# One dense stop more between the keys' transposes and the state products of the short mLSTM, and two more in its gates' chain

## The chip, the cores and the metric

The kernel runs on one core of a Trainium2 chip. The metric is device time in microseconds (us) of one launch. Engine names are those of the profile: PE is the matrix engine, PEld its weight loads, DVE the vector engine, ACT the scalar engine, POOL the general engine, SP the queue that issues most transfers. Lines (L1578) are lines of the kernel before, unless the text says that a row is from the changed kernel.

## What is computed

One hybrid encoder layer on two inputs: a prompt of 1024 tokens (sequence 0, "short") and a sample of 2048 tokens (sequence 1, "long"), each with 16 learned meta tokens in front. Width 1024, all float32, matrix products split into high and low parts (three products each).

```python
def _encoder_layer(h, ...):
    xn = _rmsnorm(h, g_pre)
    proj = xn @ w_in + b_in                       # 6672 columns
    ya = neighbourhood_attention(na_q, na_k, na_v, rpb);  ya = (ya * silu(na_z)) @ w_a
    yb = (mlstm_branch(ml_qk, ml_v, ml_g, ml_o, conv_w, head_g) * silu(ml_z)) @ w_b
    y = (sigmoid(ga) * ya + sigmoid(gb) * yb) @ w_out
    return h + _rmsnorm(y, g_post)
...
def _mlstm_chunkwise(q, k, v, ig, lf):            # per chunk, 4 heads of 128, two directions
    w = exp(a - max(a));  dC = (w * v)^T k;  dn = w k        # state products
    C, n, m = scan(C * fs + isc * dC, ...)                   # states of all chunks
    S = (q k^T) * exp(logD - m_t)                            # scores
    h = (S v + e * C q) / max(|den|, exp(-m_t))
```

## The kernel before, in words

Two streams of work are interleaved by hand on PE. The **dense** stream (`dense`) holds the big projections (`fm_half`, `tm_unit`, `sgates`) and, at the end, six blocks of merge and output projection (`final`: two for the short, four for the long sequence). It is a generator that yields after each piece of some 12 matmuls with a planned cost (`6 * C512` = 1.41 or `12 * C256` = 1.44 of the planner's microseconds). The **sparse** stream (`sparse`) runs mLSTM of the short sequence, neighbourhood attention of the short, mLSTM of the long, neighbourhood attention of the long. It yields planned costs too (`A_D` = 1.63 in the state part, `A_G` = 1.3 in the gates, times 1.15 for the short sequence), and `run` issues dense pieces until the cost is used up. So a `yield A_D` in `ml_states` is a stop at which dense work is put on PE before the next sparse instructions. Whatever dense work is left when the sparse stream ends is issued after it. PE keeps exactly this order; the other engines' orders, and that of SP, are made by a scheduler from dependencies and its own plan, so they change when PE's order does.

In `ml_states`, for each head of the mLSTM and each block of 256 tokens (four blocks and a rest of 16 tokens in the short sequence, eight and a rest in the long):

1. PE transposes the keys `kf` into PSUM (tile `tr`, L1574); ACT copies the high part `kth` (L1577), DVE subtracts for the low part `ktl` (L1578);
2. a stop; the next block's convolution and values split (`conv_b`, `vsplit`);
3. a stop; PE takes the state products (`mm3`, rows L218 to L220 with `sm<-vwh,kth`, `sm<-vwl,kth`, `sm<-vwh,ktl`), the last of each three reading `ktl`;
4. a stop, and the next block's transposes.

In `ml_gates`, `one(d)` works through a chain of small PE transposes, each of which waits for ACT or DVE work on the one before; both directions step together with a stop of `A_G`.

In `ml_outputs`, PE takes the scores (L1703, L1704) from `kh` and `kl`, which ACT (L1665) and DVE (L1666) make from the reloaded keys.

In the attention, the last products (L1288) of a row of heads are copied (L1295), added (L1302), gated (L1304) and stored by SP to a memory tile `ya` (L1305). `yload` loads it again as `yl` (L1850); ACT makes `yh` of it (L1871), DVE the low part (L1855), and `final` multiplies both (L218 to L220 with `pj<-yh`, `pj<-yl`): for each output tile first the four `yb` tiles, then the four `ya` tiles in order. The last of these four, for the last of the six blocks, comes from the very last attention work.

Other dense rows named later: L697 (DVE scales a projection's result in PSUM), L709 (ACT adds its bias), L318 (DVE makes the low part of a weight tile `whl`), L310 (SP loads a prepared weight tile), L415 and L408 (SP loads input tiles), L365 (ACT squares tokens), L534 and L542 (DVE scales and splits the input).

Of the kernel before, what the change touches and what calls it, by code (L numbers as in the profile page):

```python
# [135 lines left out]
A_N, A_D, A_A, A_G, A_S = (1.08, 0.93), 1.63, 1.79, 1.3, (1.15, 0.91)  # L136


class K:
# [1169 lines left out]
    def ml_gates(self, s, keep, mp, res):  # L1309
        nc = self.nc  # L1310
        T = SEQLEN[s]
        NC_ = 1 + T // P
        NR = 4 * NC_
        t = lambda n, sh, dt=F32, bufs=1: mp.tile(sh, dt, name=n, bufs=bufs)
        kt = lambda n: keep.tile([P, NC_, 4], F32, name=n, bufs=1)
        gt = t("g_t", [P, NC_, 16])
        for d in range(2):
            nc.gpsimd.memset(gt[:, 0, 8 * d:8 * d + 4], -BIG)
            nc.gpsimd.memset(gt[:, 0, 8 * d + 4:8 * d + 8], 1.0e4)
        nc.sync.dma_start(gt[:NM, 0, :], self.GA[s][0:NM, :])  # L1320
        nc.sync.dma_start(gt[:, 1:, :], self.GA[s][NM:, :].rearrange("(c p) g -> p c g", p=P))
        yield 11.0
        gv = gt.rearrange("p c (d k h) -> p d k c h", d=2, k=2)
        lf = t("g_lf", [P, 2, NC_, 4])
        e = t("g_e", [P, 2, NC_, 4])
        u = t("g_u", [P, 2, NC_, 4])
        fl = lambda x: x.rearrange("p d c h -> p (d c h)")
        for d in range(2):
            nc.scalar.activation(e[:, d], gv[:, d, 1], AF.Abs)
            nc.vector.tensor_scalar(lf[:, d], gv[:, d, 1], 0.0, None, op0=ALU.min)  # L1330
        nc.scalar.activation(fl(e), fl(e), AF.Exp, scale=-1.0)
        ln = t("g_ln", [P, 2, NC_, 4])
        yield A_G
        nc.vector.tensor_scalar(fl(u), fl(e), 1.0, None, op0=ALU.add)
        nc.scalar.activation(fl(ln), fl(u), AF.Ln)
        yield A_G
        nc.vector.tensor_tensor(fl(lf), fl(lf), fl(ln), op=ALU.subtract)
        nc.vector.scalar_tensor_tensor(fl(e), fl(u), -1.0, fl(e), op0=ALU.add, op1=ALU.subtract)
        nc.vector.reciprocal(fl(u), fl(u))
        nc.vector.tensor_tensor(fl(e), fl(e), fl(u), op=ALU.mult)  # L1340
        nc.vector.tensor_tensor(fl(lf), fl(lf), fl(e), op=ALU.add)
        yield A_G

        def one(d):
            l2 = lf[:, d].rearrange("p c h -> p (c h)")
            pb = self.psum("sm", [P, 512])
            nc.tensor.matmul(pb[:, :NR], self.tri[:, d, :], l2, start=True, stop=True)
            bT = t(f"g_b{d}", [P, NC_, 4])
            nc.vector.tensor_copy(bT.rearrange("p c h -> p (c h)"), pb[:, :NR])
            aT = kt(f"g_a{d}")  # L1350
            nc.vector.tensor_tensor(aT, gv[:, d, 0], bT, op=ALU.subtract)
            aTf = aT.rearrange("p c h -> p (c h)")
            yield
            pa = self.psum("sm", [P, 512])
            nc.tensor.transpose(pa[:NR, :P], aTf, self.ident)
            aR = t("g_aR", [NR, P], bufs=2)
            nc.scalar.activation(aR, pa[:NR, :P], AF.Copy)
            yield
            cm = t("g_cm", [NR, P], bufs=2)
            rv = (lambda x: x) if d == 0 else (lambda x: x[:, ::-1])  # L1360
            nc.vector.tensor_tensor_scan(out=rv(cm), data0=rv(aR), data1=rv(aR), initial=-3.0e38, op0=ALU.max, op1=ALU.max)
            end = P - 1 if d == 0 else 0
            pg = self.psum("sm", [P, 512])
            nc.tensor.matmul(pg[0:1, :NR], self.ones[:, 0:1], l2, start=True, stop=True)
            rg = t("g_rg", [1, NR], bufs=2)
            nc.scalar.activation(rg, pg[0:1, :NR], AF.Copy)
            yield
            px = self.psum("sm", [P, 512])
            nc.tensor.transpose(px[0:1, :NR], cm[:, end:end + 1], self.ident[:NR, :NR])
            ra = t("g_ra", [1, NR], bufs=2)  # L1370
            nc.vector.tensor_tensor(ra, px[0:1, :NR], rg, op=ALU.add)
            me = t("g_me", [1, NR], bufs=2)
            mpv = t("g_mp", [1, NR], bufs=2)
            nc.gpsimd.memset(mpv, 0.0)
            yield
            for h in range(4):
                w = slice(h, NR, 4)
                nc.vector.tensor_tensor_scan(out=rv(me[:, w]), data0=rv(rg[:, w]), data1=rv(ra[:, w]), initial=0.0,
                                             op0=ALU.add, op1=ALU.max)
            if d == 0:  # L1380
                nc.vector.tensor_copy(mpv[:, 4:], me[:, :NR - 4])
            else:
                nc.vector.tensor_copy(mpv[:, :NR - 4], me[:, 4:])
            yield
            pm = self.psum("sm", [P, 512])
            nc.tensor.transpose(pm[:NR, 0:1], mpv, self.ident[0:1, 0:1])
            mpc = t("g_mpc", [NR, 1], bufs=2)
            nc.vector.tensor_copy(mpc, pm[:NR, 0:1])
            uR = t("g_uR", [NR, P], bufs=2)
            nc.vector.tensor_scalar(uR, cm, mpc, -1.0, op0=ALU.max, op1=ALU.mult)  # L1390
            nc.sync.dma_start(self.UD[s][d][:, :], uR)
            uend = t("g_ue", [NR, 1], bufs=2)
            nc.vector.tensor_copy(uend, uR[:, end:end + 1])
            nc.scalar.activation(cm, uR, AF.Exp, bias=mpc)
            nc.scalar.activation(aR, aR, AF.Exp, bias=uend)
            fs = t("g_fs", [NR, 1], bufs=2)
            nc.scalar.activation(fs, uend, AF.Exp, bias=mpc)
            yield
            pu = self.psum("sm", [P, 512])
            nc.tensor.transpose(pu[:, :NR], uR, self.ident[:NR, :NR])  # L1400
            em = kt(f"g_em{d}")
            nc.vector.tensor_tensor(em.rearrange("p c h -> p (c h)"), pu[:, :NR], bT.rearrange("p c h -> p (c h)"), op=ALU.subtract)
            nc.scalar.activation(em, em, AF.Exp)
            dg = t("g_dg", [NR, NR], bufs=2)
            nc.vector.tensor_scalar(dg, self.ident[:NR, :NR], fs, None, op0=ALU.mult)
            yield
            for name, x in (("e", cm), ("w", aR)):
                pe = self.psum("sm", [P, 512])
                nc.tensor.transpose(pe[:, :NR], x, self.ident[:NR, :NR])
                eT = kt(f"g_{name}T{d}")  # L1410
                nc.vector.tensor_copy(eT.rearrange("p c h -> p (c h)"), pe[:, :NR])
                out[d][name] = eT
                yield
            pf = self.psum("sm", [P, 512])
            nc.tensor.matmul(pf[:, :NR], self.ones[:NR, :], dg, start=True, stop=True)
            fsb = kt(f"g_fb{d}")
            nc.vector.tensor_copy(fsb.rearrange("p c h -> p (c h)"), pf[:, :NR])
            out[d].update(a=aT, em=em, f=fsb)

        out = [{}, {}]  # L1420
        both = [one(d) for d in range(2)]
        while both:
            both = [x for x in both if next(x, "end") != "end"]
            yield A_G
        res += out
# [85 lines left out]
    def ml_states(self, s, h, g, NB, sts):  # L1511
# [55 lines left out]
        for i in range(N):  # L1567
# [13 lines left out]
            conv_b(i + 1)  # L1581
            vsplit(i + 1)
            yield A_D
            vwh, vwl = vws.pop(i)
            if not c0:
                pd = self.psum("sm", [P, 512])
# [10 lines left out]
            for j in range(CB - 1, -1, -1):  # L1597
# [6 lines left out]
                if cc > 0:  # L1604
                    nc.vector.scalar_tensor_tensor(sts[(cc - 1) // CB][:, (cc - 1) % CB, 130:260], sts[b][:, j, 130:260],
                                                   g[1]["f"][:, 1 + cc, h:h + 1], pd[:, 130:260], op0=ALU.mult, op1=ALU.add)
            yield A_D

    def ml_outputs(self, mp, s, h, g, NB, sts, norms):

# [596 lines left out]
```

## Time and profile before

| | us |
|---|---|
| median of 3 runs (lowest, highest) | 2678.69 (2675.17, 2685.75) |
| the profiled execution's own time | 2675.68 |
| its span on the core | 2673.9 |
| PE busy | 2637.4 |
| DVE busy | 1916.3 |
| ACT busy | 1424.9 |
| granted PE clock, mean | 0.996 |

The span runs from the first to the last instruction. PE's busy time is of interest with its idle time beside it: PE is idle for only 36.5 us in all, some 8 of them at the start. PE takes its instructions in the order of the program, so when one of them waits, all dense work behind it waits too. A row of the timeline reads: start, duration, engine, line, operation, output<-inputs, shapes, count, and in brackets the idle time of the engine before it and what ended it.

### The profile page before, as it was taken

To read this page: it belongs to the slowest core of one execution; us is meant where nothing else is said; L and a number is where in the kernel's file an instruction comes from. 1 tells how busy PE (TensorE), PEld (TensorE's weight loads), DVE (VectorE), ACT (ScalarE), POOL (GpSimd) and SP (SyncE) were. 2 spreads that over 40 slices of the span, in tenths; PEclk is the share of its full clock that TensorE was granted. 3 is DMA by queue.
4 is the path that set the end of the run, shared out by engine and by line. 5 is a ranking of instruction groups with operands and counts; after the bars stand their busy time and mean duration, and the time that the engine had idled before them with its cause. 6 is when DMAs were issued, how large, how long until landed. Compare 5 with 4: busy or idle time off the path is not lost.

```text
span 2673.9 us, 46686 instructions
## 1 busy us (share of the span) xinstructions
PE 2637.4 (99%) x15928; PEld 2329.0 (87%) x15928; DVE 1916.3 (72%) x5070; ACT 1424.9 (53%) x3292; POOL 195.7 (7%) x418
## 2 busy tenths in 40 slices
PE   9999999999999999999999999999999999999998
PEld 7998897899978999888888888887889898989888
DVE  5655678788666878546686776867478989897854
ACT  5423555554445655546665665656365655656521
POOL 0111130011301215000000000000000000000000
PEclk9999999999999999999999999999999999999999
DMA  9899988799866999978889988899899898998965
GB/s 371 330 333 337 331 294 311 276 340 312 300 228 233 355 321 306 322 227 274 259 272 344 371 285 267 267 357 337 281 312 308 285 313 276 288 308 265 343 227 207
DMA packets 393517, 800.47 MB, mean 299 GB/s; under 512 B 50528, under 2 KB 173360, under 8 KB 389440
## 3 DMA queue, kind: packets, MB, share of 16 engines
q1 hardware_dynamic: 361728, 697.24, 77.8%
q0 software_dynamic: 31552, 100.25, 10.1%
q8 instruction: 126, 2.06, 0.3%
q14 instruction: 111, 0.91, 0.1%
HBM read 543.72 MB, written 253.60 MB: 298 GB/s over the span
## 4 chain that ended last, share of the span: by engine, by line
PE 87%; DMA 7%; DVE 4%; ACT 2%; issue 1%; SPq 0%; DVEq 0%; ACTq 0%
PE pj L218 9%; PE pj L220 9%; PE pj L219 9%; PE pj L988 8%; PE pj L990 7%; PE pj L989 7%; PE pj L787 5%; PE pj L789 5%; PE pj L788 5%; PE pj L1954 3%; PE pj L1953 3%; PE pj L1955 3%; PE sm L1288 2%; PE tr L1273 2%; DMA wraw<-wu 2%; DMA whl<-w 1%
## 5 line engine op out<-in xcount | busy, mean ns | idle before, releaser
L218 PE MATMUL pj<-xh,whl 128*128 128x512 f32 (+1 forms) x960 | 369.8, 385 | 5.0 <-DMA whl<-w 3.4
L220 PE MATMUL pj<-xh,whl 128*128 128x512 f32 (+1 forms) x960 | 361.2, 376 | 0.0
L219 PE MATMUL pj<-xl,whl 128*128 128x512 f32 (+1 forms) x960 | 360.5, 375 | 0.2 <-DVE xl L446 0.2
L787 PE MATMUL pj<-whl,xh 128*128 128x256 f32 (+1 forms) x1152 | 328.9, 285 | 0.0
L789 PE MATMUL pj<-whl,xl 128*128 128x256 f32 (+1 forms) x1152 | 325.3, 282 | 0.0
L788 PE MATMUL pj<-whl,xh 128*128 128x256 f32 (+1 forms) x1152 | 324.9, 282 | 0.0
L1953 PE MATMUL pj<-whl,mh 128*128 128x256 f32 x768 | 218.1, 284 | 1.1 <-DMA whl<-w 1.1
L787 PEld LDWEIGHTS pj<-whl,xh 128*128 128x128 f32 x1152 | 217.1, 188 | 0.3
L788 PEld LDWEIGHTS pj<-whl,xh 128*128 128x128 f32 x1152 | 217.0, 188 | 0.2
L789 PEld LDWEIGHTS pj<-whl,xl 128*128 128x128 f32 x1152 | 217.0, 188 | 0.0
L1954 PE MATMUL pj<-whl,mh 128*128 128x256 f32 x768 | 216.2, 282 | 0.0
L1955 PE MATMUL pj<-whl,mlo 128*128 128x256 f32 x768 | 215.4, 280 | 0.0
L218 PEld LDWEIGHTS pj<-xh,whl 128*128 128x128 f32 x960 | 181.4, 189 | 37.1 <-issue 4.8
L220 PEld LDWEIGHTS pj<-xh,whl 128*128 128x128 f32 x960 | 181.3, 189 | 35.1
L219 PEld LDWEIGHTS pj<-xl,whl 128*128 128x128 f32 x960 | 181.8, 189 | 30.5 <-issue 1.0
L988 PE MATMUL pj<-xh,whl 128*128 128x512 f32 x512 | 206.7, 404 | 1.5 <-ACT pj L1005 1.1
L990 PE MATMUL pj<-xh,whl 128*128 128x512 f32 x512 | 202.0, 395 | 0.0
L989 PE MATMUL pj<-xl,whl 128*128 128x512 f32 x512 | 201.0, 393 | 0.0
L1280 DVE TENSOR_TENSOR pts<-tr,pts 96x384 fp32r<-96x384 f32 (+2 forms) x192 | 118.7, 618 | 63.4 <-ACT pts L1275 61.9
L1275 ACT ACTIVATE pts<-tr 96x384 fp32r<-96x384 f32 (+2 forms) x192 | 103.5, 539 | 102.6 <-PE tr L1273 101.8
L218 PE MATMUL pj<-yh,whl 128*128 128x512 f32 x384 | 154.1, 401 | 0.0
L219 PE MATMUL pj<-yl,whl 128*128 128x512 f32 x384 | 151.5, 395 | 0.7 <-DVE yl L1855 0.7
(380 smaller groups left out, 6828.8 us busy)
## 6 DMA issues: line engine op xcount, KB each, us to landing
whl<-w SPq DMA_DIRECT2D x131, 1024.0 KB
whl<-q SPq DMA_DIRECT2D x112, 512.0 KB
w<-whl SPq DMA_DIRECT2D x36, 1024.0 KB
wraw<-wu SPq DMA_DIRECT2D x48, 512.0 KB
gt<-st SPq DMA_DIRECT2D x96, 256.0 KB
tg<-gt SPq DMA_DIRECT2D x96, 256.0 KB
q<-po POOLq DMA_DIRECT2D x26, 512.0 KB, 6.8
xt<-xt SPq DMA_DIRECT2D x24, 512.0 KB
```

What stands on the lines that cost most here:

```text
L218: mm(out, ah, bh, start=start, stop=False)
L219: mm(out, ah, bl, start=False, stop=False)
L220: mm(out, al, bh, start=False, stop=stop)
L787: nc.tensor.matmul(o, xh, wh, start=k == 0, stop=False)
L788: nc.tensor.matmul(o, xh, wl, start=False, stop=False)
L789: nc.tensor.matmul(o, xl, wh, start=False, stop=k == KT - 1)
L988: mm(bank, w[:, 0, k], xh[:, k], start=fresh and k == 0, stop=False, skip_group_check=True)
L989: mm(bank, w[:, 0, k], xl[:, k], start=False, stop=False, skip_group_check=True)
L990: mm(bank, w[:, 1, k], xh[:, k], start=False, stop=k == 3, skip_group_check=True)
L1953: nc.tensor.matmul(o, mh[:, k, xs], wh, start=clear > 0 and k == 0, stop=False)
L1954: nc.tensor.matmul(o, mh[:, k, xs], wl, start=False, stop=False)
L1955: nc.tensor.matmul(o, ml[:, k, xs], wh, start=False, stop=clear < 2 and k == KT - 1)
```

## The change

All edits are for the short sequence alone (`s == 0`):

- `one(d)` in `ml_gates` stops once more before the transpose of `uR` (L1400) and once more before the transposes of `cm` and `aR` (L1409);
- `ml_states` stops twice instead of once between the next block's `vsplit` and the state products, and no longer between the state products and the next block's transposes. The last block (the rest of 16 tokens) leaves the loop by its own stop, so it has one stop more than before.

```diff
@@ ml_gates, one(d)
             nc.scalar.activation(fs, uend, AF.Exp, bias=mpc)
             yield
+            if s == 0:
+                yield
             pu = self.psum("sm", [P, 512])
...
             nc.vector.tensor_scalar(dg, self.ident[:NR, :NR], fs, None, op0=ALU.mult)
             yield
+            if s == 0:
+                yield
             for name, x in (("e", cm), ("w", aR)):
@@ ml_states
             conv_b(i + 1)
             vsplit(i + 1)
             yield A_D
+            if s == 0:
+                yield A_D
             vwh, vwl = vws.pop(i)
...
-            yield A_D
+            if s:
+                yield A_D
```

No instruction is added or taken away; instructions move. In the rows of the changed kernel the same code has higher line numbers (by 2 to 7).

**PE, the second block of head 1 in `ml_states`.** `tr<-ident,kf` are the transposes, `sm<-...` the state products, `pj<-xh,whl` and `pj<-xl,whl` dense matmuls. Before:

```order
L1574 MATMUL tr<-ident,kf 128x128 x2
L218 MATMUL pj<-xh,whl 128x512
L219 MATMUL pj<-xl,whl 128x512
L220 MATMUL pj<-xh,whl 128x512
...
L218 MATMUL sm<-vwh,kth 128x260
L219 MATMUL sm<-vwl,kth 128x260
L220 MATMUL sm<-vwh,ktl 128x260
...
L1574 MATMUL tr<-ident,kf 128x128 x2
```

Now:

```order
L1578 MATMUL tr<-ident,kf 128x128 x2
L218 MATMUL pj<-xh,whl 128x512
L219 MATMUL pj<-xl,whl 128x512
L220 MATMUL pj<-xh,whl 128x512
...
L218 MATMUL sm<-vwh,kth 128x260
L219 MATMUL sm<-vwl,kth 128x260
L220 MATMUL sm<-vwh,ktl 128x260
L1578 MATMUL tr<-ident,kf 128x128 x2
```

Between the transposes and the products stood 18 dense matmuls, now 24; between the products and the next transposes 6, now none. In head 3, whose dense matmuls are 256 columns wide, it was 24 and is 48.

**DVE, the first scores of head 0 in `ml_outputs`.** `kl<-kf,kh` makes the low part of the keys for the scores, `s<-sc` reads the scores' result. Before:

```order
L697 TENSOR_TENSOR pj<-pj,rr 128x512
L1691 SCALAR_TENSOR_TENSOR st<-st,g_fb_3124 128x130 x2
L318 TENSOR_TENSOR whl<-wraw,whl 128x1024
L579 TENSOR_TENSOR po<-pr,po 128x2x512
L1666 TENSOR_TENSOR kl<-kf,kh 128x256
L697 TENSOR_TENSOR pj<-pj,rr 128x512
L1666 TENSOR_TENSOR kl<-kf,kh 128x256
L1711 TENSOR_TENSOR s_3839<-sc,s_3839 128x256
```

Now:

```order
L697 TENSOR_TENSOR pj<-pj,rr 128x512
L1698 SCALAR_TENSOR_TENSOR st<-st,g_fb_3150 128x130
L579 TENSOR_TENSOR po<-pr,po 128x2x512
L697 TENSOR_TENSOR pj<-pj,rr 128x512
L318 TENSOR_TENSOR whl<-wraw,whl 128x1024
L1673 TENSOR_TENSOR kl<-kf,kh 128x256 x2
L1718 TENSOR_TENSOR s_3875<-sc,s_3875 128x256
```

The first `kl` stood ahead of the last L697 before the scores; now it stands behind that L697 and an L318. That L697 scales the dense result which PE finishes directly before the scores. ACT's order moves in the same way: `kh` now stands behind the bias of that same result (L709).

**PE, where the attention of the long sequence ends.** `sm<-pts,vt` are the last products of the attention, `pj<-whl,mh` the output projection of the fifth block of `final`, `pj<-yh,whl` the first products of the sixth and last. Before:

```order
L1953 MATMUL pj<-whl,mh 128x256
L1954 MATMUL pj<-whl,mh 128x256
L1955 MATMUL pj<-whl,mlo 128x256
L1288 MATMUL sm<-pts,vt 128x256 x3
L1953 MATMUL pj<-whl,mh 128x256
```

Now:

```order
L1960 MATMUL pj<-whl,mh 128x256
L1961 MATMUL pj<-whl,mh 128x256
L1962 MATMUL pj<-whl,mlo 128x256
L1288 MATMUL sm<-pts,vt 128x256 x3
L218 MATMUL pj<-yh,whl 128x512
L219 MATMUL pj<-yl,whl 128x512
L220 MATMUL pj<-yh,whl 128x512
```

Before, 84 matmuls of the fifth block still stood between the last L1288 and the first product of the sixth block; now there is none.

## Prediction

> **What bounds the kernel now.** I read the page's shares first, then the list of what PE waits for, then the timeline around each of those waits, and the windows with the granted clock there.
>
> ```profile
> span 2673.9 us, 46686 instructions
> PE 2637.4 (99%) x15928; PEld 2329.0 (87%) x15928; DVE 1916.3 (72%) x5070; ACT 1424.9 (53%) x3292; POOL 195.7 (7%) x418
> ```
>
> PE is the bound: it is busy for 2637.4 of 2673.9 us, so all waits together are 36.5 us, and some of that is the start. No matmul is added or removed, so the change can only move waits, and what the clock loses behind them. The list of PE's waits (sum, count, longest) has these rows that the change can reach:
>
> ```profile
> PE sm L220 <- DVE ktl L1578: 5.9, 5, 2.6
> PE pj L218 <- DMA whl<-w: 3.4, 1, 3.4
> PE sm L218 <- ACT kth L1577: 2.0, 2, 1.8
> PE sm L1409 <- DVE g_eT L1411: 1.0, 1, 1.0
> PE pj L219 <- DVE yl L1855: 0.7, 1, 0.7
> PE sm L1400 <- DVE g_uR L1390: 0.5, 1, 0.5
> PE sm L1409 <- DVE g_em L1402: 0.3, 1, 0.3
> ```
>
> The state products wait for the keys' parts (kth, then ktl) for 5.9 + 2.0 = 7.9 us; the gates' chain for 1.8 us. Small sums, but in head 1 the granted clock falls behind them. Timeline of its first and second block, then windows of it (length; busy time of PE, PEld, DVE, ACT, POOL; PE clock; DMA share; GB/s):
>
> ```profile
> 424.76 0.38 PE L1574 MATMUL tr<-ident,kf 128*128 128x128 f32 x2
> 430.30 0.43 DVE L1578 TENSOR_TENSOR ktl<-tr,kth 128x256 fp32r<-128x256 f32 x1
> 430.79 0.38 PE L220 MATMUL sm<-vwh,ktl 128*128 128x260 f32 x1 [1.23 <-DVE ktl L1578]
> 432.75 0.38 PE L1574 MATMUL tr<-ident,kf 128*128 128x128 f32 x2
> 439.70 0.44 DVE L1578 TENSOR_TENSOR ktl<-tr,kth 128x256 fp32r<-128x256 f32 x1
> 440.19 0.58 PE L220 MATMUL sm<-vwh,ktl 128*128 128x260 f32 x1 [2.64 <-DVE ktl L1578]
> ...
> 425.00:433.00 8.00, 6.77 (x35) 5.47 (x34) 8.00 (x18) 3.99 (x14) 0.00 (x0) 1.00 0.25 84
> 433.00:441.00 8.00, 5.36 (x25) 4.35 (x24) 8.00 (x16) 6.85 (x12) 0.53 (x1) 0.90 0.64 191
> 441.00:449.00 8.00, 8.00 (x29) 6.56 (x29) 7.57 (x19) 7.32 (x17) 0.00 (x0) 0.67 0.97 346
> ```
>
> DVE has no gap in 16 us, and ktl lies in its queue behind other work; PE waits 1.23 and 2.64 us, and then runs 8 us at 0.67 of its clock.
>
> **The change, part by part.**
>
> Price of cover. In the dense stream one 512-column matmul follows the other at 2579.19 − 2578.96 = 0.23 us (rows under "the end" below), so six are 1.4 us and 24 are 5.5 us. The 256-column ones are taken at half, 0.12 us.
>
> *The gates* get two more pieces, each of 12 matmuls (2.8 us). The waits of 0.5, 0.3 and 1.0 us are shorter than a piece: −1.8 us. A bound above is 0, if what the vector engines do for the new pieces goes ahead of the chain.
>
> *Head 1.* ktl ended 430.30 + 0.43 − 424.76 = 5.97 us after the first of these transposes began, and 439.70 + 0.44 − 432.75 = 7.39 us in the next block. The cover grows from 18 matmuls (4.1 us) to 24 (5.5) and the transposes themselves (0.38). So 5.97 is just about met, and 7.39 would leave some 1.5, but part of this lateness is PE's own: DVE's queue there held the evictions of the dense pieces that in the new order come later. I take 0.6 us as left over (bounds 0 and 1.5). The waits give 1.23 + 2.64 = 3.87 back. The clock: (1 − 0.90) × 8 + (1 − 0.67) × 8 = 3.4 us that were lost in the two windows; I take it as regained, because the wait that stands ahead of it is shortened by the most part; bound: none of it. Head 1: −3.87 − 3.4 + 0.6 = −6.7. The pieces that stood between products and transposes are now ahead of the products; nothing waits for the transposes' new place, since they read kf alone.
>
> [...]
>
> *Head 3*, with 256-column pieces, has the other ktl waits (5.9 − 3.87 = 2.0) and kth's:
>
> ```profile
> 672.85 0.39 PE L220 MATMUL sm<-vwh,ktl 128*128 128x260 f32 x1 [1.10 <-DVE ktl L1578]
> 688.07 0.42 ACT L1683 ACTIVATE v<-va 128x260 fp32r<-128x260 f32 x1 [3.55 <-DMA va<-mv]
> 688.40 0.37 ACT L1577 ACTIVATE kth<-tr 128x256 fp32r<-128x256 f32 x1
> 689.53 0.42 DVE L1578 TENSOR_TENSOR ktl<-tr,kth 128x256 fp32r<-128x256 f32 x1
> ```
>
> The third of them is a chain: ACT waited 3.55 us for a load of values, so kth came late, then ktl. Its cover grows from 24 to 48 matmuls of 0.12, by 2.8 us, against a wait of 1.8 + 0.7 = 2.5. Together 2.0 + 1.8 = 3.8 are there to gain; I take 3.4 (bounds 3.8 and, if the load slips as far as its reader, 0). No clock was lost here that I count.
>
> *The last block's extra stop.* In each of the four heads the block of 16 tokens now has a stop more of 1.63 × 1.15 = 1.87 us in the planner's measure, 7.5 in all; with the gates' two of 1.3 × 1.15 that is 10.5. So from there to the end the dense stream stands some 10 us further on against the sparse one. This moves three places.
>
> First, *head 0 in ml_outputs*. DVE and ACT now have kl and kh behind the last dense result before the scores.
>
> ```profile
> 337.67 0.40 ACT L1665 ACTIVATE kh<-kf 128x256 fp32r<-128x256 f32 x1
> 338.95 0.42 DVE L1666 TENSOR_TENSOR kl<-kf,kh 128x256 fp32r<-128x256 f32 x1
> 340.77 0.70 DVE L697 TENSOR_TENSOR pj<-pj,rr 128x512 f32<-128x512 f32 x1 [1.41 <-PE pj L220]
> 341.56 0.69 ACT L709 ACTIVATE st<-pj,bfm 128x512 f32<-128x512 f32 x1 [3.48 <-issue]
> L318 DVE TENSOR_TENSOR whl<-wraw,whl 128x1024 fp32r<-128x1024 f32 x45 | 54.8, 1222 | 31.9 <-ACT whl L317 25.8 <-DMA mq<-st 4.3 <-DMA um<-ud 1.7
> ```
>
> Before, both parts were there 1.4 us ahead of that result. Now PE ends the result and stands before the scores: L697 0.70, L709 0.69, kh 0.40 = 1.8 us to the first score; by DVE L697 0.70, L318 1.22, kl 0.42 = 2.3 to the one that reads kl, and it is a product later. Behind it on PE everything waits, DVE and ACT get nothing new meanwhile. I take +2.1; bounds 0 (if L318 slips behind, and the load of kf comes early) and 2.3 with the clock loss of a like wait, about +4.5.
>
> Second, *a weight's load*, the one DMA wait in the list.
>
> ```profile
> 788.19 0.76 PE L218 MATMUL pj<-xh,whl 128*128 128x512 f32 x1 [3.41 <-DMA whl<-w]
> 788.00:792.00 4.00, 3.81 (x11) 3.08 (x12) 0.00 (x0) 0.00 (x0) 0.00 (x0) 0.62 1.03 409
> ```
>
> The wait is 3.41 us, and the 4 us behind it go at 0.62 of the clock, another 1.5. The queues are full there (409 GB/s, share 1.03), so the same bytes arrive at the same pace and only what stands ahead of this load on SP changes: with the dense stream further on, its load is issued nearer to the tokens' loads. Bounds: all gone, −4.9; or 2 us later, +2. I take −1.5, the middle of the two.
>
> Third, *the end*. The attention of the long sequence ends on PE some 10 us later against the dense work, and its result goes by way of memory into the last block of `final`. The fifth block's 84 matmuls, which covered that way, are now ahead of it.
>
> ```profile
> 2564.08 0.52 PE L1288 MATMUL sm<-pts,vt 104*128 104x256 f32 x3
> 2567.08 0.33 SPq L1305 DMA_DIRECT2D ya<-yg  x1
> 2569.45 0.59 SPq L1850 DMA_DIRECT2D yl<-ya  x1
> 2575.93 0.62 ACT L1871 ACTIVATE yh<-yl 128x512 fp32r<-128x512 f32 x1
> 2578.96 0.40 PE L220 MATMUL pj<-yh,whl 128*128 128x512 f32 x1
> 2579.19 0.39 PE L218 MATMUL pj<-yh,whl 128*128 128x512 f32 x1
> 2579.57 0.69 DVE L1855 TENSOR_TENSOR yl<-yl,yh 128x512 fp32r<-128x512 f32 x1
> 2580.31 0.50 PE L219 MATMUL pj<-yl,whl 128*128 128x512 f32 x1 [0.73 <-DVE yl L1855]
> ```
>
> From the last product's end, 2564.60, to the issue of the load of its result are 4.85 us. The load lands no faster, I take it, than the store took before it (2569.45 − 2567.08 = 2.4), and no later than its reader began (2575.93 − 2569.45 = 6.5); then yh 0.62 and yl 0.69. The chain is 4.85 + 2.4 + 1.31 = 8.6 us to 4.85 + 6.5 + 1.31 = 12.7. PE has, of the sixth block, 21 matmuls that do not need it: 12 of the tiles of yb, 9 of the first three of ya; 21 × 0.23 = 4.8. So it waits 3.8 to 7.9 us where it waited 0.73: +3.1 to +7.2. A wait of that length costs clock besides; the two priced above cost 1.5 (behind 3.41) and 3.4: +1.5 to +3.4. I take +6, nearer to the short load, because the queues are less full there (bounds +3.1 and +10.6).
>
> *Elsewhere* the dense pieces meet the sparse stream 10 us shifted for all of the long part, where PE's remaining waits are single ones. I take 0, with ±4.
>
> Sum: −1.8 − 6.7 − 3.4 + 2.1 − 1.5 + 6 + 0 = −5.3. The profiled execution had 2675.7 us of its own, the span and 1.8 around it, so 2670.4; it stood 3.0 below the median of the runs, so **2673 us** is what I expect of the median.
>
> **The rivals.**
>
> *The end is short* (faster). The load lands in 2.4 us, no clock is lost (+3.1), the weight's wait goes with its clock (−4.9), and head 1 leaves nothing (−7.3): −1.8 − 7.3 − 3.4 + 2.1 − 4.9 + 3.1 = −12.2, and with 2 us from the ±4 elsewhere −14: 2665 (2678.7 − 14). For it: each is a bound already worked out. Against: it needs all three.
>
> *DVE is the bound in head 1* (no change). It was busy 8.00 of 8.00 us in two windows. Then the products' wait is only moved: the order saves no DVE work, PE gains the added cover of 1.4 us, and the next block's transposes meet the same backlog; the clock stays low. −1.4 in place of −6.7 gives a sum of 0, and with the upper bound at head 0, +2.4: 2679 to 2681. For it: 16 us without a gap. Against: the windows before and behind are less full (7.57), and a queue that is a few us behind is caught up by 1.4 us per block.
>
> *ACT in head 3 waits for the next tokens* (slower). With the dense stream further on, ACT's first squares of the next tokens now stand ahead of the last two kth copies; before, behind the fourth.
>
> ```profile
> 683.56 0.33 SPq L408 DMA_DIRECT2D xr<-x_sample  x1
> 689.52 0.57 SPq L408 DMA_DIRECT2D xr<-x_sample  x1
> 695.69 1.06 ACT L365 ACTIVATE xsq<-xr 128x1024 bf16<-128x1024 f32 x1 [0.99 <-DMA xr<-x_sample]
> ```
>
> Those loads are issued 6 to 7 us apart, and ACT still waited 0.99 us for the one that the first squares of 695.69 read. If each of two products waits for such a load, that is 2 × 7 = 14 us, with the clock of two long waits 2 × 3.4 = 7, less the rest of my sum's gains there: −5.3 + 3.4 + 21 = +19: about 2698. It decides where a load lands later than 48 × 0.12 = 5.8 us after the block's transposes. For it: ACT waited 3.55 us for another load in the same place. Against: the loads go out ahead of the block's end, and SP's order moves with the dense stream, so they may be issued earlier too.
>
> That the change does not do what it says I leave out: the order on PE shows the new distance in every block of the short sequence.
>
> **How the numbers follow.** My forecast has 0.44, the short end 0.30, DVE's bound 0.14, ACT's wait 0.12. A difference of 0.5% (13.4 us) is about what a measurement of this kernel can tell from no change: faster lies below 2665.3, slower above 2692.1. The short end mostly counts as faster (0.26 of its 0.30), the forecast for 0.10 (its low end: the bounds of the end and of the weight's load together); DVE's bound and most of the rest are the same; slower gets ACT's wait and 0.04 from the forecast's upper end, where the end's chain and a new wait in the long part take their bounds. So faster 0.36, same 0.48, slower 0.16. The range for 8 of 10: from 2655 (the short end with 4 elsewhere and a second wait of the long part gone) to 2692 (the forecast with the end at +10.6, head 0 at +4.5, the load at +2 and 4 elsewhere is 2688; part of ACT's wait above it). The forecast's own range is 2664 to 2684.
>
> **What would show it.** Right: PE's list has no ktl or kth wait of over 1 us in the short part and none of the gates' rows; the windows of head 1 have a PE clock of 0.9 or more; the first score of head 0 waits about 2 us for kh or kl; and at the attention's end the first products of the sixth block that read the last part of ya wait 4 to 8 us, with a clock below 0.9 behind them. Wrong: a window of head 1 at 0.67 with DVE full (DVE's bound); an L365 that waits on ACT ahead of kth in head 3; a whl wait that has grown where 3.41 us stood; or a new wait of several us in the long part, on which no term of this sum rests.

## The result, and the profile after

The changed kernel took 2713.13 us (median of 4 runs, 2711.41 to 2717.14), the kernel before 2679.19 us beside it: a ratio of 1.0128, 95% interval [1.0115, 1.0141], slower by 34 us. The prediction was 2673 us with a range to 2692, and it gave "slower" a chance of 0.16.

The page of the changed kernel, its shares:

```profile
span 2710.5 us, 46699 instructions
PE 2644.8 (98%) x15928; PEld 2333.6 (86%) x15928; DVE 1910.5 (70%) x5070; ACT 1423.5 (53%) x3292; POOL 196.4 (7%) x418
```

PE issues the same 15928 matmuls and is busy 7.4 us longer (2637.4 before): that is clock. Its mean granted clock was 0.996 before and is 0.993 now, and 2637.4 × 0.996 / 0.993 = 2645.4. The other 29 of 36.6 us are waits. The list of PE's waits (sum, count, longest):

```profile
PE sc L1710 <- ACT kh L1672: 17.1, 3, 9.7
PE sm L1288 <- DVE yg L1302: 12.5, 5, 4.5
PE sm L1288 <- ACT prb L1256: 4.2, 7, 1.2
PE pj L218 <- ACT yh L1878: 3.9, 1, 3.9
PE sm L220 <- DVE ktl L1582: 3.8, 5, 1.4
...
PE pj L218 <- DMA whl<-w: 1.9, 1, 1.9
...
PE sm L218 <- DVE cv L1453: 1.4, 1, 1.4
```

What the change aimed at did shrink: ktl from 5.9 to 3.8 us, the gates' waits of the short part are gone, whl from 3.4 to 1.9. The waits for kh, yg and yh are new or grown (2.7, 0.7 and none before; the row for prb stood at 4.1), and nearly all of that lies outside the short mLSTM. Cut into four parts at the same places of the program (the first product of the long sequence's gates, the first scores of the long attention, its last product, PE's end), the windows of the kernel before read (length; busy time of PE, PEld, DVE, ACT, POOL; PE clock; DMA share; GB/s):

```profile
0.00:1202.76 1202.76, 1184.98 (x7560) 1066.20 (x7561) 830.24 (x2000) 600.04 (x1236) 189.40 (x392) 1.00 0.87 307
1202.76:1927.21 724.45, 719.98 (x3586) 599.06 (x3587) 502.99 (x1686) 433.58 (x1146) 4.10 (x22) 1.00 0.90 301
1927.21:2564.60 637.39, 632.43 (x4125) 572.58 (x4124) 528.48 (x1247) 374.33 (x860) 2.18 (x4) 1.00 0.93 294
2564.60:2666.42 101.82, 100.03 (x661) 91.20 (x659) 51.16 (x125) 16.43 (x51) 0.00 (x0) 1.00 0.67 243
```

and of the changed kernel:

```profile
0.00:1207.06 1207.06, 1192.96 (x7608) 1073.02 (x7609) 829.76 (x2003) 599.27 (x1240) 190.22 (x392) 1.00 0.88 308
1207.06:1949.76 742.70, 722.85 (x3580) 601.06 (x3581) 500.08 (x1683) 433.84 (x1144) 4.11 (x22) 0.99 0.89 293
1949.76:2605.57 655.81, 636.97 (x4166) 577.07 (x4165) 529.71 (x1253) 376.00 (x863) 2.05 (x4) 0.99 0.92 286
2605.57:2703.05 97.48, 91.98 (x576) 82.44 (x575) 47.48 (x118) 13.88 (x44) 0.00 (x0) 0.98 0.65 233
```

Length less PE's busy time is its idle time: 17.8, 4.5, 5.0 and 1.8 us before; 14.1, 19.9, 18.8 and 5.5 now. (What is left of the 36.5 us of before, 7.5 us, lies behind PE's last matmul and not at the start: of its first 12 us PE was idle for 2.5.) So the first part gained 3.7 us of waits, the long mLSTM lost 15.4, the long attention 13.9, the end 3.7. (The counts also show the shift: 48 matmuls more in the first part, 85 fewer in the last.)

Three places carry the loss. In the long mLSTM, head 1, the timeline shows the keys' store, the dense stream's input loads, the keys' load, and the reader:

```profile
1438.42 0.40 SPq L1540 DMA_DIRECT2D kf<-kf  x1
...
1447.94 2.07 SPq L953 DMA_DIRECT2D xl<-xl  x1
1450.12 3.13 SPq L1441 DMA_DIRECT2D raw<-mq  x1
1453.34 0.98 SPq L1627 DMA_DIRECT2D kf<-kf  x1
...
1463.04 0.51 ACT L1450 ACTIVATE cv<-raw,cw 128x256 f32<-128x256 f32 x1 [4.01 <-DMA raw<-mq]
1463.45 0.41 ACT L1672 ACTIVATE kh<-kf 128x256 fp32r<-128x256 f32 x1
1463.91 0.58 PE L1710 MATMUL sc<-q,kh 128*128 128x256 f32 x1 [5.61 <-ACT kh L1672]
```

The outputs read back the keys that the states stored 15 us earlier. That load goes out behind the dense input's tiles, and kh begins 10.1 us after its issue. What kept kh by these rows is another load of the same stretch: kh stands on ACT directly behind `cv`, the next block's convolution, and ACT waited 4.01 us there for `raw`, issued at 1450.12. When the keys themselves had landed, the rows don't show. In head 3 the first kh stands on ACT behind `v` in the same way, and ACT waited 9.57 us for its load:

```profile
1796.72 2.35 SPq L1511 DMA_DIRECT2D va<-mv  x1
...
1808.48 0.42 ACT L1690 ACTIVATE v<-va 128x260 fp32r<-128x260 f32 x1 [9.57 <-DMA va<-mv]
1808.82 0.42 ACT L1672 ACTIVATE kh<-kf 128x256 fp32r<-128x256 f32 x1
...
1809.28 0.58 PE L1710 MATMUL sc<-q,kh 128*128 128x256 f32 x1 [9.71 <-ACT kh L1672]
```

In the attention the largest wait for yg has a late load of queries ahead of it; ACT and DVE stand still for 7 us and are behind when PE comes:

```profile
2317.96 0.56 SPq L1189 DMA_DIRECT2D stk<-nq  x1
...
2327.45 0.63 ACT L1208 ACTIVATE qB<-stk 64x512 fp32r<-64x512 f32 x1 [7.08 <-DMA stk<-nq]
...
2334.66 0.42 DVE L1302 TENSOR_TENSOR yg<-sm,yg 64x256 f32<-64x256 f32 x1
2335.23 0.75 PE L1288 MATMUL sm<-pts,vt 128*128 128x256 f32 x3 [4.48 <-DVE yg L1302]
```

### The profile page after: what moved, and what is told of

The parts are those of the page before. It is cut to its first block, busy times and chain, and to the rows that moved or that the text cites. A ratio compares the mean times of both kernels' runs of the same rounds, so it can differ in the third digit from the quotient of the medians.

```text
span 2710.5 us, 46699 instructions
## 1 busy us (share of the span) xinstructions
PE 2644.8 (98%) x15928; PEld 2333.6 (86%) x15928; DVE 1910.5 (70%) x5070; ACT 1423.5 (53%) x3292; POOL 196.4 (7%) x418
## 4 chain that ended last, share of the span: by engine, by line
PE 80%; DMA 10%; DVE 5%; ACT 2%; issue 1%; SPq 1%; DVEq 0%; ACTq 0%
PE pj L218 9%; PE pj L220 9%; PE pj L219 9%; PE pj L988 7%; PE pj L990 7%; PE pj L989 7%; PE pj L787 5%; PE pj L789 5%; PE pj L788 5%; PE sm L1288 2%; PE pj L1961 2%; PE pj L1960 2%; PE pj L1962 2%; PE tr L1273 2%; DMA va<-mv 1%
## 5 line engine op out<-in xcount | busy, mean ns | idle before, releaser
L218 PE MATMUL pj<-yh,whl 128*128 128x512 f32 x384 | 155.0, 404 | 3.9 <-ACT yh L1878 3.9
L220 PE MATMUL pj<-yh,whl 128*128 128x512 f32 x384 | 153.0, 398 | 0.0
```

Source lines behind the costliest of these rows:

```text
L218: mm(out, ah, bh, start=start, stop=False)
L220: mm(out, al, bh, start=False, stop=stop)
```

## The experiments

**1. The shift alone, and the distance alone.** Is it the longer distance that costs, or that the dense stream stands further on from there? Four kernels. The first keeps the order of before in the short mLSTM and adds one stop behind it:

```diff
                 yield from self.ml(s)
+                if s == 0:
+                    yield 10.5
```

> The kernel before, with one stop of 10.5 (the planner's measure) more, once, behind the short mLSTM and ahead of the short attention; nothing else. From there on PE's order is that of the changed kernel. Theory A (the time is lost in the long part, because the dense stream stands some 10 us further on against the sparse one): the waits of the changed kernel's long part come back (for kh near 1464 and 1809, for yg in the attention, for yh at the end), and the short part's gain of some 6 us is not there: +34 to +42 us, 2713 to 2721. Rival B (the longer distance itself costs, in the short part): within 5 us of the kernel before.

Measured: 2715.71 us, ratio 1.0144 [1.0129, 1.0158], +37.9 us. The waits for kh are 6.0 and 9.5 us there, those for yg 8.9 in all, and the one for yh 4.3.

The second keeps the whole change and takes the 10.5 back over the short mLSTM's outputs (`yield A_A` becomes `yield A_O[s]` in `ml_outputs`):

```diff
+A_O = (A_A - 10.5 / (1.15 * 136), A_A)
```

> The changed kernel, with the 10.5 taken back: each of the 136 stops of the short mLSTM's outputs is 0.067 smaller (1.723 in place of 1.79), so the dense stream is even with the kernel before again at the end of the short part. Theory A: the long part is that of the kernel before, and the short part's gains are left: -4 to -11 us, 2668 to 2675. Rival B (the distance itself costs): 2700 or more.

Measured: 2669.0 us, ratio 0.9968 [0.9957, 0.9980], −8.8 us. No wait for kth or ktl of over 0.3 us is left in the short part, and the long attention takes as long as before (637.39 us), by its window:

```profile
1921.93:2557.75 635.82, 632.39 (x4125) 572.51 (x4124) 528.53 (x1247) 374.17 (x860) 2.04 (x4) 1.00 0.92 294
```

The third has the longer distance without either of the added stops that shift:

```diff
             yield A_D
+            if s == 0 and c0:
+                yield A_D
             vwh, vwl = vws.pop(i)
...
-            yield A_D
+            if s:
+                yield A_D
```

> The kernel before, with the three pieces ahead of the products and none behind them, but neither the last block's extra stop nor the gates' two stops: the dense stream is never ahead. Theory A: -3 to -8 us, 2671 to 2676, with the waits for ktl in head 1 smaller. Rival B: +20 us or more.

Measured: 2671.12 us, ratio 0.9975 [0.9966, 0.9984], −6.7 us.

The fourth has the gates' two stops alone (the first two pieces of the change's diff).

> The kernel before with the gates' two stops alone: the gates' waits (1.8 us) go, and the dense stream stands 3.0 of the planner's measure further on for the rest. If the cost of the shift were proportional to it, +10 us; if it depends on which loads meet which dense transfers, anywhere between -3 and +20 us, with waits at places of their own. Rival B (the distance in the states costs): -2 us.

Measured: 2667.91 us, ratio 0.9964 [0.9952, 0.9976], −9.9 us. That is more of a gain than any case of the expectation. So the distance is a gain, the gates' stops are a gain, and the shift of 10.5 alone costs more than the whole change. Rival B fell in the first three, and in the fourth it gave −2 us. The fourth gains 8 us beyond the gates' own 1.8; if the shift of 3.0 is what gives them, which no run shows by itself, the cost does not grow in proportion to the shift.

**2. Half the shift.** As the first kernel, with `yield 5.25`.

> The kernel before with one stop of 5.25 more behind the short mLSTM (half of the 10.5 that gave +37.9 us). If the cost grows evenly between the 3.0 of the gates' stops (-8.1 us without the gates' own 1.8) and 10.5 (+37.9): about +6 us, 2684 to 2688. If it depends on single meetings of a load with a burst, as theory A has it: no such line, anywhere from -10 to +38 us, and the places that cost are seen one by one (kh near 1464 and 1809, yg, yh).

Measured: 2701.72 us, ratio 1.0083 [1.0070, 1.0096], +22.9 us; the even line gave +6. The wait for kh in head 1 is larger than with 10.5, while the attention's waits for yg are down to 0.3 us. The timeline of that place:

```profile
1462.38 3.14 SPq L953 DMA_DIRECT2D xl<-xl  x1
1465.56 2.93 SPq L1620 DMA_DIRECT2D kf<-kf  x2
...
1477.11 0.42 ACT L1665 ACTIVATE kh<-kf 128x256 fp32r<-128x256 f32 x1 [11.19 <-DMA kf<-kf]
1477.58 0.58 PE L1703 MATMUL sc<-q,kh 128*128 128x256 f32 x1 [10.99 <-ACT kh L1665]
```

Here the load of the keys stands directly behind an input tile, and it is this load that ACT waits for. So which head is hit, and which of the small loads at its start comes last, changes with the shift; in the three cases shown it is one issued behind the dense stream's input tiles.

**3. The keys' way through memory.** In the changed kernel, for the long mLSTM, the first block's keys stay in SBUF. The 16-token block's keys get a tile of their own (the line of that is left out here):

```diff
@@ ml_states, conv_b
...
+                if c0 == NM:
+                    self.kf0 = kf
@@ ml_outputs, load
-                kfs[b] = kf = self.keep.tile([P, BL], F32, name="kf", bufs=2)
-                nc.sync.dma_start(kf, self.KF[s][h][:, t0:t0 + BL])
+                if b or not s:
+                    kfs[b] = kf = self.keep.tile([P, BL], F32, name="kf", bufs=2)
+                    nc.sync.dma_start(kf, self.KF[s][h][:, t0:t0 + BL])
+                else:
+                    kfs[b] = self.kf0
```

> The changed kernel; in the long mLSTM the keys of each head's first block of 256 stay in SBUF for the outputs and are not loaded back (the 16-token block's keys get a small tile of their own). PE's order is the changed kernel's but for 4 rows. Theory M1 (the waits for kh near 1464 and 1809, 15.3 us, are the way of these keys to memory and back, behind the dense stream's input loads): both waits go, with the clock lost behind them (0.07 and 0.10 of 50 us): -15 to -24 us, 2689 to 2698. Rival M2 (kh is late because ACT and DVE are behind with other work): 2708 or more, the waits only change their name.

Measured: 2692.72 us, ratio 1.0048 [1.0036, 1.0061], 20.4 us less than the changed kernel. Neither wait for kh is left; the window of the long mLSTM (727.45 us, of which PE idle 7.2, against 742.70 and 19.9):

```profile
1207.89:1935.34 727.45, 720.24 (x3580) 599.18 (x3581) 502.38 (x1683) 431.67 (x1144) 4.10 (x22) 1.00 0.90 298
```

PE's order is the same but for 4 rows. The time is what M1 expected, and M2 falls. But the edit changes two things at once: the keys need no load, and ACT's order now has kh ahead of cv and v (kh began at 1451.36 and 1793.15, where it had begun at 1463.45 and 1808.82). So it is shown that the waits go when kh depends on none of the late loads; that the keys' own load was the one that ended them, as M1 has it, is not shown, and the rows above name raw and va. Some 15 of the 20.4 us lie in this window; another 6.6 lie in the long attention (649.23 us, against 655.81), which the edit does not touch.

**4. The attention and the end by themselves.** The whole change, the 10.5 taken back only in the outputs of the long mLSTM's last head:

```diff
+        cut = 10.5 / (0.91 * 58) if s and h == 3 else 0.0
...
-            yield A_A
+            yield A_A - cut
```

> The changed kernel; the 10.5 are taken back only in the outputs of the long mLSTM's last head (58 stops of 1.59 in place of 1.79), so the long attention and the end stand as in the kernel before. If the attention's waits for yg and the end's for yh come from how far the dense stream stands ahead there, they go (14.8 + 3.9 us less 1.4 of before, and some 4 us of clock) and the two waits for kh stay: 2690 to 2697. If they come from something carried on from the mLSTM: 2708 or more.

Measured: 2686.14 us, ratio 1.0024 [1.0012, 1.0036], 27.0 us less than the changed kernel and 4 us less than expected. The waits for kh stay, those for yg fall to one of 1.1 us, that for yh at the end is gone:

```profile
PE sc L1711 <- ACT kh L1673: 16.8, 3, 10.1
...
PE sm L1288 <- DVE yg L1302: 1.1, 1, 1.1
```

The two parts about add up: −0.80% for the keys and −1.04% for attention and end, −1.84% together, where the kernel with the whole shift taken back (comp) stands 1.60% below the changed one; what the keys' experiment gained in the attention is counted in both parts.

**5. Why the attention's loads are late.** On top of experiment 3, its loads of queries and keys leave from POOL:

```diff
+        eng = nc.gpsimd if s else nc.sync
...
-        nc.sync.dma_start(qr[0:64], self.NQ[s][pr][...])
+        eng.dma_start(qr[0:64], self.NQ[s][pr][...])
...
```

> The changed kernel with the first keys kept in SBUF, as above (2692.7 us), and the long attention's loads of queries and keys (stk<-nq, kx<-nk, kx<-nkm) issued by POOL in place of SP; PE's order is the same. Theory Q (these loads are late because they stand behind the dense stream's loads in SP's order): ACT's waits for stk in the long attention (20.7 us in the changed kernel) fall to 5 or less, PE's waits for yg (9.7 us) to 3 or less: -7 to -12 us, 2681 to 2686. Rival S (the DMA engines are full there, so that a load is late from any queue): within 4 us, 2689 to 2697.

Measured: 2680.77 us, ratio 1.0003 [0.9993, 1.0012], 12.0 us less than experiment 3. ACT waited 15.1 us for stk there and now not at all; PE's waits for yg went from 9.7 to 5.2, not to the 3 expected. The same load, first from SP (experiment 3), then from POOL:

```profile
2298.71 0.51 SPq L1189 DMA_DIRECT2D stk<-nq  x1
...
2307.89 0.63 ACT L1208 ACTIVATE qB<-stk 64x512 fp32r<-64x512 f32 x1 [7.31 <-DMA stk<-nq]
```

```profile
2283.82 0.52 POOL L1190 DMA_DIRECT2D stk<-nq  x1 [17.11 <-PE sm L1243]
2296.89 0.62 ACT L1209 ACTIVATE qB<-stk 64x512 fp32r<-64x512 f32 x1
```

POOL issues it 13.1 us ahead of its reader, SP 9.2, of which ACT waited 7.3. The DMA engines are as full (their share from 2280 to 2300 is 1.03 and 1.04), so theory Q holds for ACT's waits and S falls. The size is less sure: of the 12.5 us between the two profiles, 7.4 lie in the long attention (649.2 and 641.9 us), nearly all around the wait behind this load, and 4.7 lie ahead of it, where nothing was edited and PE's order is the same. Whether a queue of its own helps the load besides, these runs cannot tell from the earlier issue. The 3.8 us of yg that are left stand near 1970, behind the tiles of `final`'s first block; that was not tried.

**6. What beats both kernels.** The change without the last block's extra stop (`if s == 0 and c0`), so that the shift is the gates' 3.0:

> The changed kernel without the last block's extra stop in the states: the gates' two stops and the longer distance stay, and the dense stream stands 3.0 ahead in place of 10.5. The gates' stops alone gave -9.9 us, with 2.2 us of waits for ktl left in heads 1 and 3. If the two gains add: 2661 to 2666. If the distance costs anything of its own in the short part: 2668 or more.

Measured: 2667.25 us, ratio 0.9954 [0.9942, 0.9967], −13.4 us. That lies between the two cases of the expectation: by the medians the gains do not fully add (the gates alone gave −9.9, the distance −6.7, together −16.6), but the three intervals, each some 3 us to either side, do not settle it. With the first keys kept in SBUF in both sequences:

> The changed kernel without the last block's extra stop (2667.3 us), and with the first keys of each head kept in SBUF in the short and the long mLSTM. The waits for kh left there are 0.9 us: 2663 to 2668, no more than 3 us faster than without. If the loads left out also free queues for others: 2658 to 2663.

Measured: 2667.94 us, ratio 0.9956 [0.9943, 0.9968]: nothing more, as there was almost no wait for kh to take. With the long attention's loads on POOL instead:

> The changed kernel without the last block's extra stop (2667.3 us), with the long attention's loads of queries and keys on POOL. In that kernel ACT waits 8.8 us for stk, but PE only 0 to 1 us behind it. If theory Q holds and PE is the bound: ACT's waits go, PE gains 0 to 3 us, 2664 to 2668. If SP's order is shorter for the dense loads as well: below 2664.

Measured: 2665.59 us, ratio 0.9952 [0.9938, 0.9966]. It is the lowest median of all, and within the interval the same as without POOL. A wait of 5.1 us at the start of the long gates, for which the profile names no releaser, is left in both and stays unexplained.

## Why the prediction was wrong

**The step that failed** is "*Elsewhere* the dense pieces meet the sparse stream 10 us shifted for all of the long part [...] I take 0, with ±4". It cost 15.4 + 13.9 = 29.3 us of waits and much of the 7.4 us of clock (granted 0.86 from 1464 to 1480 us, 0.84 from 1810 to 1820 and 0.83 from 2330 to 2340, behind or around waits of 5.61, 9.71 and 4.48 us). The text had the shift, its size and its reach right, and gave it three places; it then took the rest as a mere re-shuffling, because the long part's waits before were small and single. The rows that would have told are in the trace of before:

```profile
1430.34 2.39 SPq L953 DMA_DIRECT2D xl<-xl  x2
...
1439.38 0.55 SPq L1620 DMA_DIRECT2D kf<-kf  x1
...
1448.90 0.42 ACT L1665 ACTIVATE kh<-kf 128x256 fp32r<-128x256 f32 x1 [2.36 <-DMA kf<-kf]
...
1809.29 0.38 PE L1703 MATMUL sc<-q,kh 128*128 128x256 f32 x1 [2.65 <-ACT kh L1665]
```

In the long mLSTM the keys' load went out at 1439.38 and its reader on ACT began at 1448.90, after 2.36 us of waiting for it, and PE's own wait for kh at 1809.29 was 2.65 us. In head 1 the input tiles (L953) had gone out some 7 us before that load; in the changed kernel they went out directly ahead of the small loads (1447.94, then 1450.12 and 1453.34). That the other places were harmless before for the same reason is likely, but not shown. A load whose reader began 9.5 us after its issue and had waited for it, in a part whose DMA share was 0.90, had a price when the streams were moved by 10 us; the prediction needed a term for each such load, and a rival made of them, where its slower rival was in head 3 of the short part.

The other steps, with the rows that decide them. In the changed kernel's short part:

```profile
345.61 0.38 PE L1710 MATMUL sc<-q,kh 128*128 128x256 f32 x1 [1.82 <-ACT kh L1672]
442.06 0.39 PE L220 MATMUL sm<-vwh,ktl 128*128 128x260 f32 x1 [0.56 <-DVE ktl L1582]
443.87 0.36 PE L218 MATMUL sm<-vwh,kth 128*128 128x260 f32 x1 [1.43 <-DVE cv L1453]
687.89 0.39 PE L220 MATMUL sm<-vwh,ktl 128*128 128x260 f32 x1 [1.39 <-DVE ktl L1582]
```

- *The gates*, −1.8: right; none of the three waits is left in the short part.
- *Head 1*, −6.7: right in kind, too large. Waits of 0.56 + 1.43 = 2.0 are left of 3.87, and the clock fell again (last section). The residual of 0.6 was too small: ktl ended 6.7 us after the first of its transposes began in the third block, and the second wait is not for a part of the keys at all: the profile puts it down to DVE's cv, a small operation of the convolution. With the shift taken back (comp) PE has no gap there at all, so DVE's bound, a rival, fell too.
- *Head 3*, −3.4: 2.7 us are left of 3.8, so −1.1. The wait of 1.39 has DVE behind it: it stood still for 5.54 us until a DMA of keys (kf<-kf) was done, and ktl came after that. ACT's squares (L365) do stand ahead of the kth of the next block, as the slower rival said, but waited for no load: the two waits there are 0.69 and 0.63 us, and not 14. The rival's price also took the loads to be issued 6 to 7 us apart; in the trace of before they go out at 683.56, 689.52, 690.66 and 693.99.
- *Head 0's scores*, +2.1: right, 1.82, for the reason given.
- *The weight's load*, −1.5: right in sign, too small. The wait of 3.41 is gone with its clock (785 to 795 us: PE busy 10.00 us at 1.00, where it was 6.81 at 0.83), which was the lower bound of −4.9; a wait of 1.90 for another weight is new at 827.93, with the clock at 1.00 behind it.
- *The end*, +6: the mechanism right, the wait near its low bound:

```profile
2605.05 0.52 PE L1288 MATMUL sm<-pts,vt 104*128 104x256 f32 x3
2611.10 0.33 SPq L1857 DMA_DIRECT2D yl<-ya  x1
2613.69 0.63 ACT L1878 ACTIVATE yh<-yl 128x512 fp32r<-128x512 f32 x1 [6.94 <-DMA yl<-ya]
2614.37 0.49 PE L218 MATMUL pj<-yh,whl 128*128 128x512 f32 x1 [3.95 <-ACT yh L1878]
...
2615.00:2625.00 10.00, 9.90 (x36) 7.97 (x37) 4.18 (x7) 1.20 (x2) 0.00 (x0) 0.83 0.51 161
```

The load landed in 2.6 us (2.4 was the short case), the wait is 3.95 in place of 0.73, and 10 us at 0.83 cost 1.7: +4.9.

So the terms that were worked out from rows of their own places came to some −8 us in the short part, where −11.3 was forecast (the kernel with the shift taken back has −8.8 in all), and +5 at the end. Measured, by the terms above: gates −1.8, head 1 −1.9 of waits and −1.7 of clock, head 3 −1.1, scores +1.8, the load −4.9 and +1.9. The term that had no row was the one that decided.

## What to carry to other kernels

A local change that leaves one of two interleaved streams further on moves every later meeting of the two. Before pricing the place that is edited, add up what the edit does to the balance of the streams, and if it isn't zero, go through every load of the later parts that has its reader close behind it; or take the difference back at the end of the edited part, which here turned +34 us into −9. Here the small loads at a stage's start were hit (5.61 and 9.71 us of PE's waits in the long mLSTM's heads 1 and 3). What helped was to keep the first block on the chip, so that its first product hung on no load (20.4 us less in experiment 3), and to issue loads from a queue on which no bulk loads stand ahead (12.0 us less in experiment 5).

## What the runs showed of the hardware that was not expected

The granted clock was seen to fall behind two waits that are short by themselves. After the 0.56 and 1.43 us of head 1, windows of the changed kernel:

```profile
438.00:446.00 8.00, 6.01 (x28) 4.82 (x28) 6.62 (x18) 7.04 (x16) 0.00 (x0) 0.91 0.92 298
446.00:454.00 8.00, 8.00 (x36) 6.54 (x35) 6.62 (x24) 4.17 (x13) 0.10 (x1) 0.88 1.03 414
```

that is 1.7 us lost to clock beside 2.0 us of waits.

The issue of a DMA on SP took 0.40 us at 1438.42 and 3.13 us at 1450.12. The DMA share around the two was much the same (1.07 from 1436 to 1440 us, 1.04 from 1450 to 1454), so the share does not tell them apart, and what made the second one long is not shown. The next load on SP went out only behind it, at 1453.34: it was late before it had begun.
